# Two layers of sixteen experts: the last expert's first product moved ahead of the fifteenth's second one

## The chip, the core and the metric

The kernel runs on one core of one Trainium2 chip. The metric is the time of one execution on the device in microseconds, the median of the runs; lower is better.

## The reference

An encoder of two layers over 512 tokens of width 1024. Each layer has a mixer (attention in the first, a gated recurrence in the second), a layer norm, a mixture of experts and another layer norm. Only the experts and what follows them matter here:

```python
def grouped_moe(x, router_w, router_bias, w1, w3, w2):
    ...
    y = jnp.zeros_like(t)
    for e in range(N_EXPERTS):
        h = jax.nn.silu(t @ w1[e]) * (t @ w3[e])
        y = y + gates[:, e:e + 1] * (h @ w2[e])
    return y.reshape(bsz, seq, d)
...
        h = layer_norm(ALPHA * h + grouped_moe(h, router_w, router_bias, *experts[layer]), *norm2[layer])
```

There are 16 experts with an inner width of 512. Each token goes to two of them, so most gates are zero.

## The kernel before

**The work of one expert.** Up to 96 tokens of an expert are gathered into one tile (`gather`, L552) and transposed on PE (`x_t`). `w13` (from L570) multiplies them with W1 and W3: the "a" job, 48 matmuls of 128 x 96 against 512 columns. `glu` makes h from the two results (SiLU on ACT L594, product on DVE L595). `h_t` transposes h with four transposes on PE (L603), and writes it as a high part H (copy on ACT, L604) and the rest L (subtraction on DVE, L605). `w2` multiplies with W2: the "b" job, 24 matmuls (L629 to L631). `scatter` multiplies with the gate while it moves the result out of PSUM (y, ACT L639), and a DMA issued on POOL adds the rows to the buffer `ybuf` in DRAM (L640).

**Precision and weights.** Every product is made of three: high times high, low times high, high times low. So each weight tile of 128 x 1024 is split on the way: `wh` by a copy on ACT (L131), `wl` by a subtraction on DVE (L132). `Stream` hands out the weights in one order for the whole layer, the order in which `moe_items` lists them from `jobs()`. SP issues their loads as slots come free (`ld_a`, L681: one chunk is two transfers of 512 KB; `ld_b`, L687: one of 1 MB). An "a" job has four chunks, a "b" job two. `conv_to` converts ahead into a ring of four tile pairs and, but for the last twelve conversions of a layer, two more. Whatever its place in the list, a chunk takes the slot that its number gives.

**The order of the jobs.** Experts count from 0. `jobs()` puts the "a" job of an expert ahead of the "b" job of the expert before, so that PE has a first product to work on while h of the last one is made. Only at the end is the order turned: ..., 14a, 13b, 14b, 15a, 15b. For expert 15 `h_t` follows its "a" job at once (L755); for the others it is called behind the "b" job before. The framework makes all semaphores; it puts the instructions of each engine in order by their place in the program and by when it reckons them ready, so a transposition can stand on PE ahead of matmuls that the program has first.

```python
                if e in (0, E - 1):
                    HT[e] = self.h_t(h2, nm)
...
            py = self.w2(st, (l, e), *HT[e], nm, LA, e == E - 1)
            if e < E - 2:
                HT[e + 1] = self.h_t(hm, f"{l}_{e + 1}")
```

H and L of `h_t` have one buffer each, so a new H waits until the "b" job before has read the old one. PSUM has two buffers for the results of `w2`.

**The end of a layer.** Expert 15's result isn't scattered. `direct` multiplies it with one-hot matrices on PE (L664, L665), which brings its rows into token order in PSUM (`pd`). The results of the others come back from `ybuf`: four DMAs issued on POOL, one for each 128 tokens, add `ybuf` to the residual tile of these tokens (`xr`, L780). A scatter to `ybuf` waits for the one before to land, and these four wait for the last scatter. `tail` then adds `pd` to each of the four tiles on DVE (L801, two halves each) and normalises it: squares on ACT (L330), gain on DVE (L809, L834), the power -1/2 on POOL (L336), bias on DVE (L813) or POOL (L819). `pd` has four PSUM buffers, two row tiles' worth. In layer 0 the order on ACT and DVE in the tail is written out by hand in `TAIL`; each finished tile is transposed for layer 1 (L1054). In layer 1 each finished tile goes to the output (L1732).

`load_ln` (L317, L318) loads the gain g and the bias b of the norm on POOL's queue; they take the two extra buffers of the ring of converted weights.

Of the kernel before, what the change touches and what calls it, by code (L numbers as in the profile page):

```python
# [24 lines left out]
E = 16  # L25
# [14 lines left out]
LA = 2  # L40
# [155 lines left out]
class K:  # L196
# [408 lines left out]
        self.last_hl = nc.vector.tensor_tensor(L, pt, H.bitcast(F32), op=ALU.subtract).ins  # L605
        return H, L

    def w2(self, st, key, H, L, nm, la, last=False):
        nc = self.nc
        py = [self.ps.tile([P, 512], F32, name=f"py{nm}{n}", tag="r")[:CAP] for n in range(2)]  # L610
        mm = []
        for fc in range(FC):
            i = st.where[(key, "w2", fc // 2)] + fc % 2
            if last:
                with self.tc.issue_after(self.last_hl):
                    st.conv_to(i + 1 + la)
            else:
                st.conv_to(i + 1 + la)
            wh, wl = st.get(i)
            for n in range(2):  # L620
                sl = slice(n * 512, (n + 1) * 512)
                mm.append((n, fc))
                mm[-1] += (wh[:, sl], wl[:, sl])
            if last and fc % 2 == 0:
                continue
            if last:
                mm.sort(key=lambda x: x[0])
            for n, c, a, b in mm:
                nc.tensor.matmul(py[n], H[:, c], a, start=c == 0, stop=False)  # L629
                nc.tensor.matmul(py[n], H[:, c], b, start=False, stop=False)  # L630
                nc.tensor.matmul(py[n], L[:, c], a, start=False, stop=c == FC - 1)  # L631
            mm = []
        return py

    def scatter(self, l, py, gate, dst, nm):
# [60 lines left out]
    def jobs(self):  # L696
        r = []
        for e in range(E):
            r += [(e, "a"), (e - 1, "b")] if e < E - 1 else [(e - 1, "b"), (e, "a")]
        return r[:1] + r[2:] + [(E - 1, "b")]  # L700

    def moe_items(self, it, l):
# [6 lines left out]
    def moe(self, l, st, hs, after, on_done):  # L709
        nc, tc = self.nc, self.tc  # L710
        self.hs = hs
        self.s2 = [self.rp.tile([P, 2], F32, name=f"s2{l}{t}", tag="s1", bufs=4) for t in range(NT)]
        st.limit = st.where["moe_end", l]
        xg, X, HT, gi = {}, {}, {}, []
        seq = [e for e in range(OV + 1)] + ["o"] + [e for e in range(OV + 1, E)]

        def gather(i):
            if seq[i] == "o":
                self.thr, self.over = self.over_begin(l)
            ix = self.over[0][:, 0:1] if seq[i] == "o" else self.idx[:, seq[i]:seq[i] + 1]  # L720
            xg[seq[i]] = self.gather(ix, i)
            gi.append(self.last_gather)

        gather(0)
        port = self.rp.tile([P, 1], F32, name=f"port{l}", tag="port")
        with tc.issue_after(gi[0]):
            nc.gpsimd.memset(port, 0.0)
            gather(1)
        X[0] = self.x_t(xg[0], f"{l}_0")
        gather(NXG)  # L730
        first = st.where["moe", l]
        with tc.issue_after(self.last.ins), tc.issue_after(self.last_sig):
            free = nc.vector.tensor_copy(self.rp.tile([P, 1], F32, name=f"free{l}", tag="port"), port).ins
            with tc.issue_after(free):
                st.conv_to(first + 6)
        hm = None
        for e, what in self.jobs():
            nm = f"{l}_{e}"
            if what == "a":
                if e == OV:  # L740
                    self.over_count(l)
                pp = self.w13(st, (l, e), *X[e], nm, LA if e != OV else HX)
                if e == OV:
                    self.overflow(l, xg["o"])
                    tc.no_sync_barrier()
                h2 = self.glu(*pp, nm)
                if e == OV:
                    X[e + 1] = self.x_t(xg[e + 1], f"{l}_{e + 1}")
                elif e < E - 1:
                    with tc.issue_after(self.last_mm):  # L750
                        X[e + 1] = self.x_t(xg[e + 1], f"{l}_{e + 1}")
                if e + 1 + NXG < len(seq):
                    gather(e + 1 + NXG)
                if e in (0, E - 1):
                    HT[e] = self.h_t(h2, nm)  # L755
                hm = h2
                if 4 <= e < 4 + NT:
                    with tc.issue_after(gi[e]):
                        nc.gpsimd.tensor_scalar(hs[e - 4], hs[e - 4], ALPHA, 1.0, op0=ALU.mult, op1=ALU.mult)
                continue  # L760
            if e == E - 1:
                st.load_to(st.chunk(st.limit - 1) + 1)
                if l == 0:
                    self.early = True
                    st.load_to(st.nd + 2)
                    self.early = False
            py = self.w2(st, (l, e), *HT[e], nm, LA, e == E - 1)
            if e < E - 2:
                HT[e + 1] = self.h_t(hm, f"{l}_{e + 1}")
            if e == 0:  # L770
                with tc.issue_after(gi[1]), tc.issue_after(self.last.ins):
                    self.route_end()
            gate = self.gpos[:, e:e + 1]
            if e < E - 1:
                self.scatter(l, py, gate, self.dst[:, e:e + 1], nm)
                if e == E - 2:
                    g, b = self.load_ln(l, 2, ("vh", HX), self.hl2)
        acc = []
        for t in range(NT):
            acc.append(nc.gpsimd.dma_start(hs[t], self.ybuf[l][t * P:(t + 1) * P], accum_op=ALU.add).ins)  # L780
        after()
        done = st.limit
        st.limit = len(st.parts)
        if l == 0:
            st.conv_to(done + 2)
            with tc.manual_schedule(engines={mybir.EngineType.Activation, mybir.EngineType.DVE}):
                self.tail(l, py, gate, self.idx[:, E - 1:E], g, b, on_done, lambda n: st.conv_to(done + n))
        else:
            self.tail(l, py, gate, self.idx[:, E - 1:E], g, b, on_done)
# [967 lines left out]
```

## Time and profile before

| | us |
|---|---|
| median of 3 runs | 1131.86 |
| lowest, highest | 1131.6, 1134.7 |
| the profiled execution | 1139.46 |
| its span, first to last instruction | 1137.5 |

The profile is of one execution, somewhat slower than the median. Times in its views count from the first instruction. PE is TensorE (PEld its weight loads), ACT ScalarE, DVE VectorE, POOL GpSimd, SP the engine that issues loads. A matmul of 512 columns is shown with about 0.39 us though the next starts 0.23 us after it, since they are pipelined. In a timeline the bracket behind a row is how long the engine had been idle and what ended that; it is inferred, and a transfer that several semaphores stand for can be named wrongly. In the chain of waits "issue" is time in which the engine waited for nothing that the profile shows. The view of DMA issues gives the median time from issue to landing of the transfers that fall in its window. Layer 0's experts end at about 572 us of the span, layer 1's at about 1111.

### The profile page before, as it was taken

To read this page: it belongs to the slowest core of one execution; us is meant where nothing else is said; L and a number is where in the kernel's file an instruction comes from. 1 tells how busy PE (TensorE), PEld (TensorE's weight loads), DVE (VectorE), ACT (ScalarE), POOL (GpSimd) and SP (SyncE) were. 2 spreads that over 40 slices of the span, in tenths; PEclk is the share of its full clock that TensorE was granted. 3 is DMA by queue.
4 is the path that set the end of the run, shared out by engine and by line. 5 is a ranking of instruction groups with operands and counts; after the bars stand their busy time and mean duration, and the time that the engine had idled before them with its cause. 6 is when DMAs were issued, how large, how long until landed. Compare 5 with 4: busy or idle time off the path is not lost. (4 is left out here: it accounts for less than half of the span.)

```text
span 1137.5 us, 14945 instructions
## 1 busy us (share of the span) xinstructions
PE 1044.2 (92%) x5010; PEld 765.1 (67%) x5010; DVE 906.9 (80%) x1481; ACT 766.1 (67%) x1112; POOL 240.8 (21%) x238
## 2 busy tenths in 40 slices
PE   7999898995999999999979999995999999998992
PEld 5677677883677777776558657774677777775651
DVE  5586778558999999997886597848999999996775
ACT  5456688333878888786744899233878888786762
POOL 1113555315123111120210000014123111120132
PEclk9898999996999999999979999996999999999996
DMA  8181010696999999989953203496999999997983
GB/s 298 56 259 38 1 38 1 229 344 208 358 327 365 361 357 359 357 306 361 311 127 120 70 14 111 155 380 206 359 316 375 362 358 365 365 335 248 332 254 101
DMA packets 132980, 281.22 MB, mean 247 GB/s; under 512 B 8905, under 2 KB 32617, under 8 KB 132769
## 3 DMA queue, kind: packets, MB, share of 16 engines
q1 hardware_dynamic: 121344, 245.20, 60.0%
q0 software_dynamic: 10928, 33.93, 12.3%
q10 hardware_dynamic: 624, 1.08, 0.3%
q8 instruction: 41, 0.67, 0.2%
q14 instruction: 43, 0.34, 0.1%
HBM read 261.41 MB, written 23.74 MB: 251 GB/s over the span
## 5 line engine op out<-in xcount | busy, mean ns | idle before, releaser
L132 DVE TENSOR_TENSOR wl<-rr,wh 128x1024 fp32r<-128x1024 f32 x180 | 212.1, 1219 | 17.3 <-ACT wh L131 16.3
L131 ACT CAST wh<-rr 128x1024 fp32r<-128x1024 f32 x180 | 180.2, 1049 | 40.2 <-PE p L587 33.0
L132 DVE TENSOR_TENSOR wl<-rf,wh 128x1024 fp32r<-128x1024 f32 x104 | 124.0, 1220 | 20.8 <-ACT wh L131 20.3
L131 ACT CAST wh<-rf 128x1024 fp32r<-128x1024 f32 x104 | 105.2, 1048 | 46.6 <-DMA rf<-l_w_out 26.0
L132 DVE TENSOR_TENSOR wl<-raw,wh 128x1024 fp32r<-128x1024 f32 (+1 forms) x101 | 119.1, 1207 | 16.9 <-ACT wh L131 16.9
L131 ACT CAST wh<-raw 128x1024 fp32r<-128x1024 f32 (+1 forms) x101 | 100.9, 1033 | 30.5 <-PE ppx L1073 8.1
L583 PE MATMUL p<-wh,xh 128*96 128x512 f32 x256 | 103.3, 404 | 1.5 <-ACT xh L566 1.5
L629 PE MATMUL py<-wh,hh 128*96 128x512 f32 x256 | 101.4, 404 | 3.0 <-ACT y L639 1.9
L630 PE MATMUL py<-wl,hh 128*96 128x512 f32 x256 | 101.5, 396 | 1.6 <-DVE wl L132 1.6
L631 PE MATMUL py<-wh,hl 128*96 128x512 f32 x256 | 101.1, 398 | 0.9 <-DVE hl L605 0.9
L585 PE MATMUL p<-wh,xh 128*96 128x512 f32 x256 | 101.2, 395 | 0.3
L587 PE MATMUL p<-wh,xl 128*96 128x512 f32 x256 | 101.4, 396 | 0.0
L584 PE MATMUL p<-wl,xh 128*96 128x512 f32 x256 | 101.3, 396 | 0.0
L586 PE MATMUL p<-wl,xh 128*96 128x512 f32 x256 | 101.0, 395 | 0.0
L588 PE MATMUL p<-wh,xl 128*96 128x512 f32 x256 | 101.0, 395 | 0.0
L640 POOL DMA_INDIRECT ybuf<-y,dst x30 | 58.9, 1964 | 178.5 <-ACT y L639 151.8
L552 POOL DMA_INDIRECT xg<-hbuf,idx x32 | 35.4, 1108 | 237.3 <-PE xt L565 199.6
L132 DVE TENSOR_TENSOR wl<-rx,wh 128x1024 fp32r<-128x1024 f32 x56 | 66.3, 1219 | 8.4 <-ACT wh L131 8.4
L131 ACT CAST wh<-rx 128x1024 fp32r<-128x1024 f32 x56 | 56.2, 1050 | 9.8 <-PE p L587 9.1
L629 PEld LDWEIGHTS py<-wh,hh 128*96 128x96 f32 x256 | 41.4, 163 | 19.8 <-ACT y L639 3.4
L631 PEld LDWEIGHTS py<-wh,hl 128*96 128x96 f32 x256 | 41.7, 163 | 19.2 <-DVE hl L605 1.8
L585 PEld LDWEIGHTS p<-wh,xh 128*96 128x96 f32 x256 | 41.5, 162 | 19.3 <-ACT wh L131 1.2
(426 smaller groups left out, 2438.9 us busy)
## 6 DMA issues: line engine op xcount, KB each, us to landing
rr<-l_w SPq DMA_DIRECT2D x124, 512.0 KB, 11.3
rf<-l_w SPq DMA_DIRECT2D x68, 512.0 KB, 13.1
rr<-l_w SPq DMA_DIRECT2D x28, 1024.0 KB, 14.2
rx<-l_w SPq DMA_DIRECT2D x36, 512.0 KB, 12.0
raw<-l_w SPq DMA_DIRECT2D x36, 512.0 KB, 13.2
rf<-l_w SPq DMA_DIRECT2D x15, 1024.0 KB, 12.6
raw<-l_w SPq DMA_DIRECT2D x13, 1024.0 KB, 8.5
raw<-l_w_in SPq DMA_DIRECT2D x11, 1024.0 KB, 5.6
```

The costliest lines, as they stand in the source:

```text
L131: nc.scalar.copy(h[:, :w], r[:, a:a + w])
L132: nc.vector.tensor_tensor(l[:, :w], r[:, a:a + w], h[:, :w].bitcast(F32), op=ALU.subtract)
L583: nc.tensor.matmul(p1, H[:, kc], w1h[:, sl], start=f, stop=False)
L584: nc.tensor.matmul(p1, H[:, kc], w1l[:, sl], start=False, stop=False)
L585: nc.tensor.matmul(p3, H[:, kc], w3h[:, sl], start=f, stop=False)
L586: nc.tensor.matmul(p3, H[:, kc], w3l[:, sl], start=False, stop=False)
L587: nc.tensor.matmul(p1, L[:, kc], w1h[:, sl], start=False, stop=e)
L588: self.last_mm = nc.tensor.matmul(p3, L[:, kc], w3h[:, sl], start=False, stop=e).ins
L629: nc.tensor.matmul(py[n], H[:, c], a, start=c == 0, stop=False)
L630: nc.tensor.matmul(py[n], H[:, c], b, start=False, stop=False)
L631: nc.tensor.matmul(py[n], L[:, c], a, start=False, stop=c == FC - 1)
L640: nc.gpsimd.indirect_dma_start(out=self.ybuf[l], out_offset=bass.IndirectOffsetOnAxis(ap=dst, axis=0), in_=y, in_offset=None, bounds_check ...
```

## The change

The list of jobs keeps one order to the end: ..., 14a, 13b, 15a, 14b, 15b. Expert 15's `h_t` moves with it. It can't run ahead of 14b in the buffers of `h_t`, since expert 14's H and L are in use, so it takes the tiles of x (tags `xh` and `xl`, by the tag "x"), and it is called by a function that `w2` calls behind half of expert 14's matmuls. As the loads follow the list, the weights of 15a are loaded and converted ahead of those of 14b.

```diff
@@ w2
-    def w2(self, st, key, H, L, nm, la, last=False):
+    def w2(self, st, key, H, L, nm, la, last=False, mid=None):
...
             mm = []
+            if fc == 1 and mid:
+                mid()
         return py
@@ jobs
-            r += [(e, "a"), (e - 1, "b")] if e < E - 1 else [(e - 1, "b"), (e, "a")]
+            r += [(e, "a"), (e - 1, "b")]
         return r[:1] + r[2:] + [(E - 1, "b")]
@@ moe
-                if e in (0, E - 1):
+                if e == 0:
                     HT[e] = self.h_t(h2, nm)
...
-            py = self.w2(st, (l, e), *HT[e], nm, LA, e == E - 1)
+            def mid():
+                if e == E - 2:
+                    HT[E - 1] = self.h_t(hm, f"{l}_{E - 1}", "x")
+
+            py = self.w2(st, (l, e), *HT[e], nm, LA, e == E - 1, mid)
```

## Rows read from the trace of the kernel before

**Rows 1.** The page, busy time of each engine: us, share of the span, instructions.

```profile
PE 1044.2 (92%) x5010; PEld 765.1 (67%) x5010; DVE 906.9 (80%) x1481; ACT 766.1 (67%) x1112; POOL 240.8 (21%) x238
```

**Rows 2.** Chain that ended last, at layer 1's end: start us, us, what.

```profile
1093.69 6.23 DMA ybuf<-y,dst
1104.07 13.83 issue
```

**Rows 3.** Timeline of POOL, both layers' ends: start us, us, engine, line, what.

```profile
556.74 2.36 POOL L640 DMA_INDIRECT ybuf<-y,dst  x1 [3.04 <-ACT wh L131]
566.14 3.62 POOL L780 DMA_DIRECT2D xr<-ybuf  x4 [7.03 <-DMA ybuf<-y,dst]
...
1084.76 1.41 POOL L640 DMA_INDIRECT ybuf<-y,dst  x1 [12.92 <-DMA rr<-l_w]
1093.69 2.48 POOL L640 DMA_INDIRECT ybuf<-y,dst  x1 [2.90 <-ACT wh L131]
1100.44 3.62 POOL L780 DMA_DIRECT2D xr<-ybuf  x4 [4.27 <-DMA ybuf<-y,dst]
```

**Rows 4.** Layer 0: DMA issues, us to landing; the third accumulation's issue on POOL.

```profile
ybuf<-y,dst POOLq DMA_INDIRECT x1, 8.9
...
xr<-ybuf POOLq DMA_DIRECT2D x1, 512.0 KB, 5.4
...
567.27 2.49 POOL L780 DMA_DIRECT2D xr<-ybuf  x2
...
xr<-ybuf POOLq DMA_DIRECT2D x3, 512.0 KB, 9.4
```

**Rows 5.** The same of layer 1, ahead of them expert 13's scatter.

```profile
ybuf<-y,dst POOLq DMA_INDIRECT x1, 8.1
...
xr<-ybuf POOLq DMA_DIRECT2D x1, 512.0 KB, 5.5
...
1101.60 2.47 POOL L780 DMA_DIRECT2D xr<-ybuf  x2
...
xr<-ybuf POOLq DMA_DIRECT2D x3, 512.0 KB, 9.3
```

**Rows 6.** Timeline of DVE: first sums of the tail that use a row tile.

```profile
577.44 0.68 DVE L801 SCALAR_TENSOR_TENSOR xr<-xr,pd 128x512 f32<-128x512 f32 x1
...
1111.77 0.69 DVE L801 SCALAR_TENSOR_TENSOR xr<-xr,pd 128x512 f32<-128x512 f32 x1 [0.59 <-PE pd L665]
1115.24 0.68 DVE L801 SCALAR_TENSOR_TENSOR xr<-xr,pd 128x512 f32<-128x512 f32 x1
```

**Rows 7.** Timeline of PE, both layers' ends; in brackets idle time and its releaser.

```profile
545.61 0.39 PE L631 MATMUL py<-wh,hl 128*96 128x512 f32 x1
...
572.28 0.39 PE L664 MATMUL pd<-yh,ot 96*128 96x512 f32 x1
...
1077.29 0.47 PE L630 MATMUL py<-wl,hh 128*96 128x512 f32 x1 [0.82 <-DVE wl L132]
...
1082.64 0.39 PE L631 MATMUL py<-wh,hl 128*96 128x512 f32 x1
1083.96 0.47 PE L629 MATMUL py<-wh,hh 128*96 128x512 f32 x1 [0.93 <-ACT y L639]
...
1089.68 0.39 PE L583 MATMUL p<-wh,xh 128*96 128x512 f32 x1
...
1100.64 0.39 PE L588 MATMUL p<-wh,xl 128*96 128x512 f32 x1
1101.88 0.55 PE L603 MATMUL ht<-call,hm 96*128 96x96 f32 x4 [0.85 <-DVE hm L595]
...
1110.88 0.39 PE L664 MATMUL pd<-yh,ot 96*128 96x512 f32 x1
```

**Rows 8.** Windows of layer 1: us, busy (count) by engine, PEclk, DMA share, GB/s.

```profile
1083.00:1089.80 6.80, 5.88 (x26) 3.99 (x26) 5.67 (x6) 5.86 (x9) 2.04 (x2) 1.00 1.04 395
1105.00:1108.00 3.00, 3.00 (x8) 1.94 (x8) 1.83 (x2) 0.00 (x0) 0.00 (x0) 0.50 1.02 195
```

## The prediction

> **What bounds the kernel now.** I read the page first: PE is the busiest engine, 92% of the span [rows 1]. That is the share over the whole kernel, and it says nothing yet of a layer's end, so I went to the chain that ended last. There, at layer 1's end, it leaves PE: a transfer into `ybuf` of 6.2 us, the issue of the loads that add `ybuf` to the row tiles, and then 13.8 us in which the chain names no engine at all [rows 2]. So I followed that path by hand, with POOL's timeline and the DMA issues.
>
> The path is: y of expert 14, its scatter, the landing of that scatter, four accumulating loads (L780), and the tail's sums (L801). POOL issues the scatter at 556.74 in layer 0 and 1093.69 in layer 1, and the first accumulating load at 566.14 and 1100.44, in both cases released by the landing of that scatter [rows 3]. The scatter took 8.9 us in layer 0 [rows 4] and 6.2 in layer 1 [rows 2]; 0.5 us lie between landing and next issue. The first accumulation lands 5.4 and 5.5 us after its issue. The third is issued at 567.27 and 1101.60, 1.1 and 1.2 us after the first; the view that holds the last three gives a median, so the middle one, of 9.4 and 9.3 us [rows 4, 5]. It is there at 576.7 and 1110.9, that is 10.5 us after the first issue in both layers. The tail's sums are one row tile after the other on DVE, in a fixed order in layer 0, and the third tile's first sum runs at 577.44 and 1115.24 [rows 6]. **So the slack of this path is only 0.8 us in layer 0 and 4.3 in layer 1.** PE's path to the same sums runs through expert 15: its transposes, second product and the products `pd`, which begin at 572.28 and 1110.88 [rows 7]. In layer 1 the first sum waited for `pd` (0.59 us) while its row tile, due at 1100.44 + 5.5 = 1105.9, had been there for 5.9 us [rows 3, 5, 6].
>
> **The change part by part.** *What goes.* Expert 15's transposes no longer stand behind its own first product. In layer 1, PE idles 0.85 us before them and the whole step takes from 1100.64 to beyond 1101.88 + 0.55 [rows 7]. Expert 14's second product no longer waits 0.93 us behind expert 13's for y to leave PSUM [rows 7], since expert 15's first product stands between them.
>
> *What moves.* Expert 14's second product (24 matmuls), and with it its y, its scatter and all that waits for that, go behind expert 15's first product (48). In expert 15's, 47 steps take 1100.64 - 1089.68 = 10.96 us, 0.233 each [rows 7]. After the last matmul of expert 13 at 1082.64 come 72 matmuls (16.8 us), and four transposes (0.55 at most), so the last matmul of expert 14 is issued at 1100.0 if nothing waits. It will wait: at the head of expert 15's first product for conversions that ACT begins only after y and the copy of H, and at the head of expert 14's second for a conversion behind SiLU and the gate product. The nearest row of the second kind is the 0.82 us at 1077.29, behind expert 14's first product; there eight transposes of x stood in front, which nothing replaces now (by the four at 1101.88 up to 1.1 us, so up to 1.9 in all). The nearest of the first kind is the 0.93 us at 1083.96 [rows 7], with two conversions already done in both cases. The lower end is no wait at all, since the conversions may be ahead: 0 to 2.8 us. I take 0.9 for the second, as in its row, and 0.5 for the first, half of its row: 1.4. From the last matmul to the scatter's issue expert 13 needs 1084.76 - 1082.64 = 2.1 us [rows 3, 7], with the copy of H ahead of y; here that copy is done earlier, so 1.6 to 2.1, and I take 1.8. The scatter is then issued at 1100.0 + 1.4 + 1.8 = 1103.2, **9.5 us later than now** (7.9 to 11.2). In layer 0 the same count from 545.61 gives 566.2, 9.4 later than 556.74.
>
> *What hides it.* Now the scatter has a start of one whole first product on the tail, and that cover is what the change takes. A wait that goes with it doesn't help: expert 13's scatter lands 8.1 us after 1084.76, at 1092.9, and that is what holds expert 14's until 1093.69, though the releasers named there are a conversion and a weight [rows 3, 5]; after the change it has long landed, and the 9.5 us have that in them.
>
> *Layer 0.* The scatter took 8.9 us beside the loads of the next weights, and 6.2 in layer 1 where these had ended [rows 2, 4]. Ten us later the loads have ended here too, so I take 7.0 (6.2 to 8.9). Landing 573.2, first issue 573.7, third tile 584.2: the third tile's sum goes from 577.44 to 584.2, **6.8 us later**. With both ends (issue 564.5 and landing after 6.2; 567.9 and 8.9) it is 4.2 to 10.4. What stands behind that sum on DVE, the first normalised tile and layer 1's first products, follows in the same order, and I take the delay as handed on in full.
>
> *Layer 1.* Scatter 6.2 us, landing 1109.4, first issue 1109.9, third tile 1120.4 instead of 1115.24: **5.1 us later**. At the low end DVE fills its wait for the third tile with the normalisation of the first; then only the first tile's slack counts: 1101.6 + 6.2 + 0.5 + 5.5 = 1113.8 against 1111.77, 2 us. At the high end (issue 1104.9, landing after 8.9) it is 9.6.
>
> *What costs nothing.* The transposes in the middle of expert 14's second product: ACT's copy and DVE's subtraction have the other half of that product as cover; without it they would be the wait that stands there now. Expert 15's H and L go into the tiles of x, free once its first product has ended. SP's queue: expert 15's four chunks of W1 and W3 (eight transfers) go ahead of expert 14's two of W2, of the same size, into slots that come free at the same places; what covers this is their lead: PE's waits here name ACT and DVE, none a transfer [rows 7], and if it failed one landing would come on top of the 1.4 us. POOL's queue: the loads of g and b come free by the same places in the stream of conversions as now, and stay ahead of the scatter; the four accumulations stay behind it, and nothing else waits on POOL but the tail's small powers, which are later with everything.
>
> The sum is 6.8 + 5.1 = 11.9 us. The profiled execution took 1139.46, so it would take 1151.4; the median of the runs lies 7.6 us lower, so 1131.86 + 11.9 = 1143.8.
>
> One price I weigh against a rule. While only the accumulations run the DMA engines are full (share 1.02) at 195 GB/s, where weight loads moved 395 [rows 8]; I take the 195, because it is this transfer at this place. The Trainium skill (DMA: Bandwidth & Descriptors, Anatomy of one DMA) gives a fixed 2.0 us and 436 GB/s instead: three loads would then be an estimated 5.6 us, and the sum 2.1 instead of 11.9. The rows' 10.5 us disagree with it.
>
> **The rivals.** *PE sets the end, and it gets faster.* Expert 15's second product would begin with no transposes, copy or subtraction before it. By the count above `pd` begins at 1100.2 + 1.4 + 24 x 0.233 + 0.5 (half of the 0.93, y alone) = 1107.7 instead of 1110.88, and in layer 0 at 570.7 instead of 572.28; together 4.8 us, time 1127.1. Part of it is the clock: from 1105 to 1108, behind the idle stretches, it was granted at 0.50, the 1.2 GHz level [rows 8]. The Trainium skill (TensorE: Matmul & The Clock Gate, Why this matters for your kernels) asks to leave no idle gaps between bursts of matmuls, which speaks for this change. This rival decides only if the scatter and three accumulations took under 9 us after 1103.2, not the 17 that they take. 0.09.
>
> *The accumulations are fast when alone.* If they moved at the 395 GB/s of the weight loads, the third would be there 2.8 us (5.5 less 0.52 MB at 195 GB/s) + 3 x 1.33 = 6.8 after the first issue instead of 10.5, and each layer would lose 3.7 less: 1136.4, slower still. The Trainium skill's rule above would make that 1134.0. For it speaks that the engines can move twice as much; against it, that the accumulations had them to themselves from 1105 to 1108, with the weights in. 0.04.
>
> *The order on PE does not change*, because instructions are put on a queue by readiness as well as by place. Then expert 14's scatter stays where it is, 1131.9. Against it: expert 14's second product and expert 15's first now stand on PE in the order of the program, 1083.96 and 1089.68 [rows 7]. 0.07.
>
> **How the numbers follow.** About 0.3% (3.4 us) is what a measurement can tell from no change. My case has 0.80, all of it slower by over 0.3%; its low ends of both layers give 1138 (4.2 + 2.0) and its high ends 1152 (10.4 + 9.6), and as two high ends hardly fall together I stop at 1150. Fast accumulations add 0.04 to slower: 0.84. No change has 0.07, faster 0.09. The range reaches down to 1134, past the fast accumulations, and leaves out the faster case and most of no change.
>
> **What would show it.** In the changed trace: the scatter of expert 14 issued near 566 and, with the delay of layer 0 taken off, 1103; accumulations issued some 7 us after it and landing 2.5 us apart; the tail's first sums waiting for a DMA and no longer for `pd`; PE idle before `pd` of the third tile; expert 15's second product at one pace, begun at once. I am wrong if the accumulations land before `pd` is there, or if the third tile's sum in layer 0 is less than 3 us later.

## The result, and the profile after

| | before | after |
|---|---|---|
| median, us | 1131.73 (1131.44 to 1134.7, 4 runs) | 1146.24 (1143.57 to 1149.06, 4 runs) |
| ratio, after to before | | 1.0105 (95%: 1.0068 to 1.0142) |
| the profiled execution, span | 1137.5 | 1141.6 |

The change makes the kernel slower, by 1.05% (11.9 us of 1131.7; the interval is 7.7 to 16.1). The ratio is not the quotient of the two medians, which lie 14.5 us apart. The prediction was 1143.8, 11.9 more than the median shown to it.

The two spans can't be set against each other as they stand: the place of the change is reached at different times (layer 0's expert 13 ends at 545.61 in the profile of before [rows 7], at 540.98 in that of after, and between 540.2 and 546.0 in all profiles of the study, with either order). So every time below is counted **from the last matmul of expert 13's second product** in its layer.

The page, busy time of each engine, first row as in [rows 1]. PE is busy for 4 us less (a second profile of the kernel before has 1041.4, so 2.8 of them need no edit) and the kernel is slower, so PE's share of 91% again says nothing about the layer's end:

```profile
PE 1040.0 (91%) x5010; PEld 762.2 (67%) x5010; DVE 906.5 (79%) x1481; ACT 765.9 (67%) x1112; POOL 241.0 (21%) x238
```

POOL's timeline at both layers' ends (start us, us, engine, line, what; in brackets idle time and its releaser). It answers to [rows 3]:

```profile
542.87 1.43 POOL L642 DMA_INDIRECT ybuf<-y,dst  x1 [17.89 <-ACT y L641]
...
561.54 1.54 POOL L642 DMA_INDIRECT ybuf<-y,dst  x1 [13.01 <-ACT y L641]
567.41 3.62 POOL L786 DMA_DIRECT2D xr<-ybuf  x4 [4.33 <-DMA ybuf<-y,dst]
...
1087.43 1.41 POOL L642 DMA_INDIRECT ybuf<-y,dst  x1 [14.95 <-DMA rf<-l_w]
...
1105.96 1.56 POOL L642 DMA_INDIRECT ybuf<-y,dst  x1 [12.87 <-ACT y L641]
1111.84 3.62 POOL L786 DMA_DIRECT2D xr<-ybuf  x4 [4.32 <-DMA ybuf<-y,dst]
```

Expert 14's scatter now follows expert 13's by 18.7 us (561.54 - 542.87), where it followed by 9.0 (556.74 [rows 3] - 547.73; in layer 1 by 8.9 [rows 3]). In layer 0 the accumulating loads start 26.4 us after expert 13's last matmul (567.41 - 540.98) instead of 20.5 (566.14 - 545.61).

DMA issues (us from issue to landing) in layer 0: the scatter of 14, the load of the next mixer's weights issued at 566.88, and the first accumulating load; then the first one of layer 1. They answer to [rows 4, 5]:

```profile
ybuf<-y,dst POOLq DMA_INDIRECT x1, 5.3
...
raw<-l_w_in SPq DMA_DIRECT2D x1, 1024.0 KB, 5.8
...
xr<-ybuf POOLq DMA_DIRECT2D x1, 512.0 KB, 8.0
...
xr<-ybuf POOLq DMA_DIRECT2D x1, 512.0 KB, 5.4
```

The scatter is faster than in either layer before (8.9 and 6.2 us), the first accumulation of layer 0 slower (8.0 instead of 5.4). What stands beside it is the load of `l_w_in`. The view of the DMA queues (packets, MB, share of the 16 DMA engines' time; q1 carries SP's loads, q0 what POOL issues) has from 569 to 571.5 us that load alone:

```profile
q1 hardware_dynamic: 732, 0.75, 99.8%
```

So the accumulation, issued at 567.41, moves nothing until the load is nearly through; in layer 1, with nothing beside it, its first packets go under 2 us after its issue. In the kernel before the two stand the other way round. There the same load is issued at 572.49, behind the four accumulations, and it is the load that takes long (9.7 us to landing instead of 5.8):

```profile
raw<-l_w_in SPq DMA_DIRECT2D x1, 1024.0 KB, 9.7
```

DVE's timeline, the tail's sums (L807) and, in layer 1, the gain of the first tile (L815). It answers to [rows 6]:

```profile
575.52 0.69 DVE L807 SCALAR_TENSOR_TENSOR xr<-xr,pd 128x512 f32<-128x512 f32 x1 [7.35 <-DMA xr<-ybuf]
...
577.98 0.69 DVE L807 SCALAR_TENSOR_TENSOR xr<-xr,pd 128x512 f32<-128x512 f32 x1 [0.90 <-DMA xr<-ybuf]
...
580.50 0.69 DVE L807 SCALAR_TENSOR_TENSOR xr<-xr,pd 128x512 f32<-128x512 f32 x1 [0.92 <-DMA xr<-ybuf]
...
602.10 1.29 DVE L1064 TENSOR_TENSOR x<-ftm,x 128x512 fp32r<-128x512 f32 x2 [3.82 <-ACT x L1063]
...
1117.33 0.69 DVE L807 SCALAR_TENSOR_TENSOR xr<-xr,pd 128x512 f32<-128x512 f32 x1 [4.88 <-DMA xr<-ybuf]
...
1119.74 0.69 DVE L807 SCALAR_TENSOR_TENSOR xr<-xr,pd 128x512 f32<-128x512 f32 x1 [0.86 <-DMA xr<-ybuf]
...
1120.97 1.28 DVE L815 SCALAR_TENSOR_TENSOR xr<-xr,lw,g 128x1024 f32<-128x1024 f32 x1
...
1122.35 0.68 DVE L807 SCALAR_TENSOR_TENSOR xr<-xr,pd 128x512 f32<-128x512 f32 x1
```

This view has the main result. Before, the first sum waited for `pd`, in layer 1 for 0.59 us [rows 6] and in layer 0 for 0.50:

```profile
574.45 0.69 DVE L801 SCALAR_TENSOR_TENSOR xr<-xr,pd 128x512 f32<-128x512 f32 x1 [0.50 <-PE pd L665]
```

Now it waits 7.35 us in layer 0 and 4.88 us in layer 1 for a row tile to come back from `ybuf`, and in layer 0 the second and third sum wait again, 2.5 us apart, the pace at which the accumulations land. In layer 1 DVE takes the first tile's gain ahead of the third tile's sum, so that sum waits for nothing.

PE's timeline, which answers to [rows 7]:

```profile
540.98 0.39 PE L631 MATMUL py<-wh,hl 128*96 128x512 f32 x1
...
553.44 0.70 PE L629 MATMUL py<-wh,hh 128*96 128x512 f32 x2 [0.33 <-ACT wh L131]
553.98 0.53 PE L603 MATMUL ht<-call,hm 96*128 96x96 f32 x4
555.09 0.47 PE L630 MATMUL py<-wl,hh 128*96 128x512 f32 x1 [0.58 <-DVE wl L132]
...
560.02 0.39 PE L631 MATMUL py<-wh,hl 128*96 128x512 f32 x1
560.73 0.47 PE L629 MATMUL py<-wh,hh 128*96 128x512 f32 x1 [0.32 <-ACT y L641]
...
566.36 0.49 PE L666 MATMUL pd<-yh,ot 96*128 96x512 f32 x1
...
576.27 0.80 PE L666 MATMUL pd<-yh,ot 96*128 96x512 f32 x1 [7.11 <-DVE xr L807]
...
1085.55 0.39 PE L631 MATMUL py<-wh,hl 128*96 128x512 f32 x1
...
1110.80 0.50 PE L666 MATMUL pd<-yh,ot 96*128 96x512 f32 x1
```

PE has done what the change wants: short gaps (0.32 to 0.58 us), expert 15's second product right behind expert 14's. But then it idles 7.11 us before `pd` of the third row tile, whose PSUM buffer the first tile's sum has to free. Windows of PE's clock (us, busy and count by engine, PEclk, DMA share, GB/s): layer 0 while only the accumulating loads move, then the restart in layer 1's mixer, then layer 1's last products, which answer to the last of [rows 8]:

```profile
572.60:580.40 7.80, 3.75 (x8) 2.31 (x8) 3.10 (x11) 2.03 (x3) 0.57 (x1) 0.50 1.07 211
...
592.30:598.30 6.00, 6.00 (x27) 5.78 (x28) 5.97 (x7) 2.31 (x3) 0.00 (x0) 0.50 0.01 3
598.30:604.00 5.70, 5.70 (x50) 5.70 (x49) 1.90 (x3) 1.07 (x2) 0.55 (x1) 1.00 1.01 351
...
1105.00:1108.00 3.00, 2.85 (x12) 2.02 (x13) 1.96 (x3) 2.56 (x4) 1.56 (x1) 1.00 0.00 0
```

Before, the same restart stood at the 1.2 GHz level for 3.2 us only; the same view of before:

```profile
589.20:592.40 3.20, 3.20 (x13) 2.98 (x14) 3.20 (x4) 2.33 (x3) 0.00 (x0) 0.50 0.00 0
592.40:598.00 5.60, 5.60 (x49) 5.60 (x48) 2.91 (x5) 0.74 (x2) 0.55 (x1) 0.98 0.50 148
```

And DVE's timeline of before, the landmark that answers to 602.10 above:

```profile
597.88 1.29 DVE L1058 TENSOR_TENSOR x<-ftm,x 128x512 fp32r<-128x512 f32 x2 [2.69 <-ACT x L1057]
```

**Where the time went.** In layer 0 the third tile's sum goes from 31.83 us (577.44 - 545.61 [rows 6, 7]) to 39.52 (580.50 - 540.98): 7.7 later. By the third tile's features in the next mixer, a landmark behind the slow clock, it is 52.27 (597.88 - 545.61) to 61.12 (602.10 - 540.98): 8.85. The 1.15 between them is the clock's: 27 matmuls ran at the low level instead of 13. An estimate from the windows, 14 matmuls at 6.00 / 27 = 0.22 us instead of 5.70 / 50 = 0.11, gives 1.5 us; it is somewhat high, since short transposes are among the 50. In layer 1 the third tile's sum is 4.2 later (32.60 to 36.80), but the end of the span only 1.2 (54.86 to 56.05). Both are larger against a second profile of the kernel before, 5.8 (from 31.01) and 2.7 (from 53.33); why is said under "Both kernels again".

### The profile page after: what moved, and what is told of

Same layout as the page of the kernel before. It is cut to its first block, busy times and chain, and to the rows that moved or that the text cites. A ratio compares the mean times of both kernels' runs of the same rounds, so it can differ in the third digit from the quotient of the medians.

```text
span 1141.6 us, 14949 instructions
## 1 busy us (share of the span) xinstructions
PE 1040.0 (91%) x5010; PEld 762.2 (67%) x5010; DVE 906.5 (79%) x1481; ACT 765.9 (67%) x1112; POOL 241.0 (21%) x238
## 5 line engine op out<-in xcount | busy, mean ns | idle before, releaser
L629 PE MATMUL py<-wh,hh 128*96 128x512 f32 x256 | 99.1, 401 | 1.4 <-ACT wh L131 0.8
L585 PEld LDWEIGHTS p<-wh,xh 128*96 128x96 f32 x256 | 41.6, 163 | 20.4 <-ACT wh L131 2.4
L630 PEld LDWEIGHTS py<-wl,hh 128*96 128x96 f32 x256 | 41.3, 161 | 19.7 <-DVE wl L132 4.6
L583 PEld LDWEIGHTS p<-wh,xh 128*96 128x96 f32 x256 | 41.6, 163 | 18.4 <-ACT xh L566 2.4
## 6 DMA issues: line engine op xcount, KB each, us to landing
rr<-l_w SPq DMA_DIRECT2D x30, 1024.0 KB, 14.3
raw<-l_w SPq DMA_DIRECT2D x36, 512.0 KB, 13.1
rf<-l_w SPq DMA_DIRECT2D x15, 1024.0 KB, 12.5
```

Source lines behind the costliest of these rows:

```text
L583: nc.tensor.matmul(p1, H[:, kc], w1h[:, sl], start=f, stop=False)
L585: nc.tensor.matmul(p3, H[:, kc], w3h[:, sl], start=f, stop=False)
```

## The experiments

The table has all the kernels that ran, each beside runs of the kernel before on the same chip. "Layer 0" is the time from expert 13's last matmul to the third tile's features (L1058 of before), "layer 1" that from expert 13's last matmul to the end of the span, each of the profiled execution. Layer 1's 1.5 us of spread in the order of before (53.3 to 54.9) is there without any edit. The kernel before gave 1.0019 against itself, so a ratio this close to 1 says little.

| kernel | median, us | ratio to before (95%) | layer 0 | layer 1 |
|---|---|---|---|---|
| before, the first profile | | | 52.27 | 54.86 |
| before again | 1137.6 | 1.0019 (0.9997 to 1.0040) | 52.77 | 53.33 |
| after, the first profile | 1146.24 | 1.0105 (1.0068 to 1.0142) | 61.12 | 56.05 |
| after again | 1149.06 | 1.0128 (1.0092 to 1.0164) | 61.13 | 56.40 |
| layer 0 alone | 1148.03 | 1.0110 (1.0083 to 1.0137) | 60.94 | 54.92 |
| layer 1 alone | 1137.58 | 1.0027 (1.0005 to 1.0049) | 52.28 | 56.40 |
| no scatter of 14 | 1133.35 | 0.9984 (0.9958 to 1.0011) | 58.01 | 50.07 |
| before, accumulations late | 1147.8 | 1.0129 (1.0082 to 1.0176) | 61.70 | 57.25 |
| transposes behind 14b | 1148.33 | 1.0120 (1.0076 to 1.0164) | 60.94 | 56.42 |
| third w_in load behind | 1140.56 | 1.0053 (1.0032 to 1.0074) | 58.40 | 53.27 |
| the same again | 1138.62 | 1.0031 (1.0018 to 1.0044) | 58.29 | 53.27 |
| both experts on PE | 1137.84 | 1.0022 (1.0004 to 1.0040) | 52.50 | 52.10 |
| both on PE, loads gated | 1132.47 | 0.9976 (0.9962 to 0.9991) | 52.49 | 52.13 |

### Both kernels again

No edit; the two show what a repeat is worth.

> The kernel before, unchanged. It measures how far two sets of runs of one kernel lie apart and gives a second profile of it. Theory (the 4.1 us between the two profiled spans is too little because the first profiled execution of before lost 5 us in its first 130 us): ratio 1.000 within 0.3%, and a span near 1130, with the third row tile's sum of layer 0's tail at most 1 us behind the landing of its accumulation. Rival (the tail's times in that execution were untypical too): the tail's sums stand elsewhere against the last matmul of expert 13 than 31.8 us (layer 0) and 32.6 us (layer 1).

> The changed kernel, unchanged. Theory (a late scatter of expert 14 in both layers): 1.008 to 1.013 times the kernel before, and again the first sums of both tails wait for an accumulation, the scatter issued 20.5 us after the last matmul of expert 13. Rival (its slower runs are another effect, for instance of the clock): the time moves by over 0.4% from run to run with the tails unchanged.

The difference stands: 1.0019 against 1.0128. Before and after lie 8.4 to 8.9 us apart in layer 0, by which pair of profiles is taken, and 1.2 to 3.1 in layer 1. The span of before was not near 1130, as was expected, but 1135.4; its expert 13 too ends late in layer 0, at 545.94.

The rival of the first expectation holds for layer 1: there the third tile's sum comes 31.01 us after expert 13's last matmul, not 32.6, and `pd` begins after 26.67 us instead of 28.24. That is PE's clock. The stretch that stood at 0.50 in the first profile [rows 8] is granted 1.00 in this one, behind the same three gaps on PE (0.85, 0.57 and 0.45 us):

```profile
1105.00:1108.00 3.00, 3.00 (x14) 2.09 (x13) 1.26 (x2) 0.43 (x1) 0.00 (x0) 1.00 1.07 206
```

So the first profile's figures for layer 1, on which the prediction rests too, have some 1.5 us of slow clock in them that this kernel does not always have.

### One layer at a time

`jobs` takes the layer and keeps the old end of the list in the other one (shown for layer 0 alone):

```diff
-            r += [(e, "a"), (e - 1, "b")]
+            r += [(e, "a"), (e - 1, "b")] if e < E - 1 or l == 0 else [(e - 1, "b"), (e, "a")]
...
-                if e == 0:
+                if e == 0 or (e == E - 1 and l != 0):
...
-                if e == E - 2:
+                if e == E - 2 and l == 0:
```

> The new order in layer 0 alone, layer 1 as before. Theory from the changed trace (layer 0 loses 7.7 us in its tail and 1.1 us behind it): 1131.7 + 8.8 = 1140.5. Rival, the terms as they were forecast (6.8): 1138.5. Rival, the loss is shared evenly by the layers: 1139. A time within 2 us of the whole change would say that layer 1's end costs nothing.

> The new order in layer 1 alone, layer 0 as before. Theory from the changed trace (the third row tile's sum is 4.2 us later, of which the tail takes back all but 1.2): 1132.9. Rival, the forecast term (5.1 us, the tail handing it on): 1136.8. Rival (PE's gain of 3 us reaches the end): 1128.7.

Layer 0 alone has all of the loss that a ratio can show (1.0110 of 1.0105 to 1.0128), layer 1 alone 0.27%, with an interval that begins just above none, and the kernel before gave 0.19% against itself. The traces order the layers in the same way: +8.2 to +8.7 us in layer 0, +1.5 to +3.1 in layer 1. The ratio of layer 0 alone is more than that, 12.5 us (9.4 to 15.5) where 8.8 were expected; where the rest lies was not found out.

### No scatter of expert 14

```diff
-                self.scatter(l, py, gate, self.dst[:, e:e + 1], nm)
+                self.scatter(l, py, gate, self.dst[:, e:e + 1], nm, e != E - 2)
...
+        if not send:
+            return
```

> The order after, with the scatter of expert 14's rows left out (its two products and the scaling of y stay, so TensorE does the same work; the output lacks expert 14's rows). Theory (the wait for the scattered rows 14 is the whole loss): the accumulating loads wait for expert 13's scatter alone, which is issued some 20 us before 14's was, so the first sum of the tail waits for TensorE's pd instead of the accumulations: DVE's 7.35 us wait (layer 0) and 4.88 us wait (layer 1) are gone, the tail's sums start near 568 and 1113 us on the clock of the profile after, and the time falls to or a little under the kernel before: ratio to the kernel before 0.995 to 1.000. Rival (the new order itself costs time on TensorE, by its three short gaps per layer or its clock): the ratio stays at 1.010 to 1.013.

The ratio falls to 0.9984: **with TensorE's order that of after, the kernel as a whole loses nothing once nothing waits for that scatter.** So the order on PE isn't the cause. In the profile of layer 0, though, most of the loss is still there, by another wait: the sums don't begin near 568 us, as was expected. POOL, ACT, PE and DVE of that kernel, in that order:

```profile
551.61 3.59 POOL L788 DMA_DIRECT2D xr<-ybuf  x4 [3.09 <-DMA ybuf<-y,dst]
...
568.89 1.99 ACT L131 CAST wh<-raw 128x1024 fp32r<-128x1024 f32 x2 [5.77 <-DMA raw<-l_w_in]
570.78 1.25 ACT L660 ACTIVATE yh<-py,gpos 96x512 fp32r<-96x512 f32 x2
...
571.52 2.22 PE L668 MATMUL pd<-yh,ot 96*128 96x512 f32 x4 [5.04 <-ACT yh L660]
...
574.20 0.69 DVE L809 SCALAR_TENSOR_TENSOR xr<-xr,pd 128x512 f32<-128x512 f32 x1 [0.56 <-PE pd L669]
```

The wait that was taken away made room for another one. The accumulations, issued at 551.61, now move beside the two `w_in` loads that were issued at 537 and 540. From 558 to 568 us the queues of that kernel moved:

```profile
q0 software_dynamic: 490, 1.75, 87.9%
q1 hardware_dynamic: 380, 0.38, 13.5%
```

The plain loads, which have the engines nearly to themselves in the window above from after, get 13.5% here. ACT waits 5.77 us for the first of them, and behind that conversion on ACT's queue stands yh, without which PE can't begin `pd`. Layer 0 is 58.0 instead of 52.3; layer 1, which has no such loads, is 50.1, 3.3 to 4.8 us shorter than before, and the two nearly cancel. The profiled execution is the second slowest of the ten (1137.62, median 1133.35), so ACT's wait may be less in others. That layer 0 loses nothing with PE's new order and no scatter of 14 is seen in the kernels with both experts on PE, below: 52.5.

### The order of before, with late accumulations

A second scatter, of a tile of zeros to the same rows, behind that of expert 14:

```diff
+        if again:
+            z = self.wp.tile([CAP, D], F32, name="yz" + nm, tag="y", bufs=3)
+            nc.vector.memset(z, 0.0)
+            nc.gpsimd.indirect_dma_start(
+                out=self.ybuf[l], out_offset=bass.IndirectOffsetOnAxis(ap=dst, axis=0), in_=z, in_offset=None,
+                bounds_check=S + CAP - 1, oob_is_err=True, compute_op=ALU.add)
```

> The order before, with one scatter more: a tile of zeros added to expert 14's rows behind the scatter of 14, so that the accumulating loads start some 5 to 9 us later (one scatter took 5.4 to 8.9 us) while TensorE's order is that of before. Theory (a late start of the accumulations is what costs): the third tile's sum of layer 0, which had 0.8 us to spare, comes 4 to 8 us later, that of layer 1, with 4.3 us to spare and a tail that can put other work ahead, 0 to 2 us, and the clock of the next stage gives up to 1 us more: ratio to the kernel before 1.004 to 1.009. Rival (order on TensorE is the cause): ratio 0.998 to 1.002.

POOL and DVE of that kernel:

```profile
561.95 1.81 POOL L646 DMA_INDIRECT ybuf<-yz,dst  x1 [7.38 <-DVE wl L132]
568.05 3.64 POOL L786 DMA_DIRECT2D xr<-ybuf  x4 [4.29 <-DMA ybuf<-yz,dst]
...
576.50 0.69 DVE L807 SCALAR_TENSOR_TENSOR xr<-xr,pd 128x512 f32<-128x512 f32 x1 [7.20 <-DMA xr<-ybuf]
```

This is the loss without the change: the jobs stand in the order of before, the accumulations start 27.0 us after expert 13's last matmul (568.05 - 541.04; 26.4 in after), DVE waits 7.20 us, and the ratio is after's, 1.0129. The mechanism is what was expected; the size was put too low (1.004 to 1.009), because here too the first accumulation took over 8 us (568.05 to 576.50) instead of 5.4, beside a load of `w_in` that was issued at 567.85.

### Transposes behind expert 14's second product

```diff
-            py = self.w2(st, (l, e), *HT[e], nm, LA, e == E - 1, mid)
+            py = self.w2(st, (l, e), *HT[e], nm, LA, e == E - 1)
+            mid()
```

> The order after, with expert 15's transposes behind the whole of 14b, as in the order of the other experts, not in its middle. Theory (TensorE does not set the end, the accumulating loads do): 15b and pd come about 1.5 to 2.5 us later in each layer, which stays inside the 7.35 and 4.88 us that DVE waits for the loads: the time is that of after, ratio to the kernel before 1.009 to 1.014, and the waits shrink by what pd is later. Rival (TensorE sets the end): 3 to 5 us more than after, ratio 1.013 to 1.017.

The time is after's, but that tells nothing of PE: the transposes (L603) stand at 12.99 us from expert 13's last matmul here and at 13.00 in after (553.98 - 540.98), at the head of 14b in both. Their place on PE is not set by where the program calls them. So the test doesn't tell the theories apart; it is one more repeat of after. That the diff's "middle" isn't where they run is read from the timeline above.

### The next mixer's load behind the accumulations

The third chunk of `w_in` goes on POOL's queue, behind the four accumulating loads:

```diff
-                nc.sync.dma_start(t.rearrange("p (a b) -> p a b", a=KC),
+                q = nc.gpsimd if c0 == D + 512 else nc.sync
+                q.dma_start(t.rearrange("p (a b) -> p a b", a=KC),
...
             st.conv_to(done + 2)
+            self.early = True
+            st.load_to(st.nd + 1)
+            self.early = False
```

> The order after, with the third chunk of the next mixer's weights (1 MB) sent from GpSimd's queue behind the four accumulating loads of layer 0, instead of from SyncE's queue, where it was issued at 566.88 us and moved beside them. Theory (that load is why layer 0's first accumulation took 8.1 us from its issue where it takes 5.4 us alone): DVE's wait of 7.35 us in layer 0 shrinks to 4.5 to 5.2 us, the third tile's sum comes 2 to 3 us earlier, and the time is 2 to 3 us under after: ratio to the kernel before 1.006 to 1.011. Rival (the accumulations are slow there of themselves, after the scatter): the wait stays over 7 us and the ratio is after's, 1.010 to 1.013. Layer 1 is not touched.

> The same kernel as the one with the third w_in load behind the accumulations, once more: its time stood 6 to 8 us under after's by the ratios, while the traces show 2.7 us of it in layer 0. If the trace has it all, the ratio to before is 1.007 to 1.010; if the earlier ratio holds, 1.003 to 1.0075.

POOL and DVE of layer 0:

```profile
568.45 3.65 POOL L786 DMA_DIRECT2D xr<-ybuf  x4 [4.52 <-DMA ybuf<-y,dst]
570.66 2.39 POOL L915 DMA_DIRECT2D raw<-l_w_in  x1
...
573.98 0.69 DVE L810 SCALAR_TENSOR_TENSOR xr<-xr,pd 128x512 f32<-128x512 f32 x1 [4.95 <-DMA xr<-ybuf]
```

With the load out of the way the first accumulation is there after 5.5 us (568.45 to 573.98, was 8.1), DVE's wait is 4.95 instead of 7.35, and layer 0 is 2.7 us shorter. **So the loads of the next stage are why layer 0's accumulations were slower than before.** In the kernel before, the same chunk was issued at 572.49, 6.3 us behind the first accumulation; from expert 13's last matmul that is 26.9 us, against 25.9 in after. The change moves the accumulations, hardly the load, and so puts them side by side. The Trainium skill (DMA: Bandwidth & Descriptors, Queues, rings and completion order) says that each DMA engine takes turns between the queues that have work for it. By that both transfers should be late; the rows show it for one only, the one that came second: in after the accumulation (8.0 instead of 5.4), while the load took 5.8, against a median of 5.7 for the eight loads of its line; in before the load (9.7). In the run without the scatter, where both have long been under way, the queues sent 490 and 380 packets in the same time; that looks like turns, with more bytes and far more time for a packet of an accumulation.

The ratio fell by more than 2.7 us: 1.0053 and 1.0031 against 1.0105 and 1.0128. Of what is left, 3.0 us lie at the very end. The last instruction on DVE:

```profile
1131.22 1.28 DVE L822 SCALAR_TENSOR_TENSOR xr<-xr,lw,b 128x1024 f32<-128x1024 f32 x1 [0.66 <-POOL lw L336]
```

The row ahead is DVE's timeline; the span and clock of the core are:

```profile
core 0: 1136.5 us, clock 0.960
```

From there to the end it is 5.3 us, in both profiles of this kernel; in after it is 8.3 us (1133.29 to 1141.6), and so, within 0.5 us, in all other kernels of the study. What shortens it was not found out; the load on POOL's queue alone doesn't, since the gated kernel below has it too and ends 8.2 us behind.

### Both experts on PE

Expert 14's result goes the way of expert 15's: split, and added by one-hot products into the same `pd`. No scatter of 14, and no row left out:

```diff
-                self.scatter(l, py, gate, self.dst[:, e:e + 1], nm)
+                if e < E - 2:
+                    self.scatter(l, py, gate, self.dst[:, e:e + 1], nm)
+                else:
+                    self.d14 = self.direct(py, gate, self.idx[:, e:e + 1], nm, 0)
...
-                nc.tensor.matmul(ps, oh[:, t], yH[:, sl], start=True, stop=False)
-                nc.tensor.matmul(ps, oh[:, t], yL[:, sl], start=False, stop=True)
+                for i, (oh, yH, yL) in enumerate(parts):
+                    nc.tensor.matmul(ps, oh[:, t], yH[:, sl], start=i == 0, stop=False)
+                    nc.tensor.matmul(ps, oh[:, t], yL[:, sl], start=False, stop=i == len(parts) - 1)
```

The second of the two kernels also holds layer 0's accumulations until both `w_in` loads have landed, and has the third `w_in` load on POOL's queue, as above:

```diff
+            gate_ins = nc.gpsimd.tensor_tensor(lit, st.raw[c0][:, 0:1], st.raw[c0 + 1][:, 0:1], op=ALU.add).ins
+        with tc.issue_after(gate_ins):
             for t in range(NT):
                 acc.append(nc.gpsimd.dma_start(hs[t], self.ybuf[l][t * P:(t + 1) * P], accum_op=ALU.add).ins)
```

> The order after, with expert 14's rows brought in the same way as expert 15's: its y split into a high and a low part and added by one-hot products on TensorE into the same pd, and no scatter of 14 (16 matmuls more per layer; every row is computed). Theory: the accumulating loads of layer 0 start near 551 us, as in the run without the scatter, and there collide with the two w_in loads that were issued at 537 and 540 us, so ScalarE's conversion of w_in waits and holds yh and pd back behind it (5.8 us in that run): DVE's wait for xr is gone, one for PE of 4 to 7 us stands in its place, and the time is that of the kernel before plus up to 4 us for the 16 matmuls per layer: ratio 0.998 to 1.004. Rival (the accumulations were the only thing in the way, and the collision is an accident of one execution): pd starts at 566 to 568 us and the ratio is 0.994 to 0.998.

> As the kernel with both experts on TensorE, and in layer 0 the accumulating loads are held on GpSimd until the two w_in loads have landed (a one-column add that reads both), and the third w_in load goes behind them on the same queue. Theory: w_in lands at 557 to 560 us as in after, the conversion and yh are not held, the accumulations run alone from about 560 us (first sum possible at 565.5, third at 570.6), pd comes at 566.5 to 569: no wait over 2 us is left on DVE in front of the tail's sums, the third tile's sum comes 0 to 2.5 us earlier than in before against the last matmul of 13b: ratio to the kernel before 0.995 to 1.000. Rival (something else holds the tail: the 16 matmuls more, or DVE's extra split of y for expert 14, 2 x 0.7 us, ahead of weight conversions): ratio 1.001 to 1.006.

POOL and DVE of the gated one, layer 0:

```profile
560.66 0.18 POOL L805 TENSOR_TENSOR landed<-raw,raw 128x1 f32<-128x1 f32 x1 [12.90 <-DMA raw<-l_w_in]
561.14 3.64 POOL L808 DMA_DIRECT2D xr<-ybuf  x4 [0.30 <-POOL landed L805]
...
569.14 0.69 DVE L833 SCALAR_TENSOR_TENSOR xr<-xr,pd 128x512 f32<-128x512 f32 x1
...
572.22 0.68 DVE L833 SCALAR_TENSOR_TENSOR xr<-xr,pd 128x512 f32<-128x512 f32 x1
```

No sum waits for a DMA any more, and at 0.9976 this version beats before and after. Its gain isn't where it was expected: the third tile's sum of layer 0 comes 31.98 us after expert 13's last matmul (572.22 - 540.24), as before (31.83), and the 1.2 to 2.7 us are in layer 1 (52.13). Without the gate the ratio is 1.0022, within what was expected. Its accumulations, too, move beside the `w_in` loads (14.3 us from issue to landing in the median), but the wait that was to explain the ratio is not in its profile: ACT waits for no `w_in` there, and its two stages are as long as the gated one's. That profile is of the fastest of its six executions (1132.31, median 1137.84). The 0.46% between these two is thus open; the 5.77 us wait of the run without the scatter is one candidate, if it comes in some executions and not in others.

## Why the prediction was right

**The path, right.** The prediction followed y of 14, scatter, landing, four accumulations, sums. Taking the scatter away takes the loss away (0.9984 in all; in layer 0 by the kernels with both experts on PE, 52.5), and delaying the accumulations alone, with the old order, brings it about (1.0129). The first rival, PE sets the end, falls with these two; but its arithmetic held: `pd` begins 25.25 us after expert 13's last matmul in layer 1 (1110.80 - 1085.55) and 25.38 in layer 0, where it said 25.1 for both. The 4.8 us that it gave to PE are simply not on the path. Layer 1's last products ran at the 2.4 GHz level now (1.00 from 1105 to 1108, where it was 0.50 [rows 8]). The Trainium skill's wish for no idle gaps (TensorE: Matmul & The Clock Gate, Why this matters for your kernels) would have that so, but no run here shows that the change did it: the second profile of the kernel before has the gaps and 1.00 as well. In the old order the stretch is slow in two profiles of four, in the new one in none of seven.

**When the scatter is issued, right.** "9.5 us later than now", 20.56 us after expert 13's last matmul: measured 20.56 in layer 0 (561.54 - 540.98) and 20.41 in layer 1. The parts differ a little. The last matmul of 14b comes 19.04 us after that point, where 18.8 was said; from there to the scatter it is 1.52, not 1.8. That the parts add up so well is luck: the 0.5 us of wait at the head of 15a did not come, but 15a itself took 0.4 to 0.6 longer. The transposes of expert 15 ran at the head of 14b, not in its middle, as their call has it; their cover was only longer by that.

**The scatter, too slow in the sum.** Layer 0 was given 7.0 us and took 5.3; layer 1 was given 6.2 and took 5.4. It had the DMA engines to itself in both.

**The accumulations of layer 0, too fast in the sum: the mis-sized term.** The prediction took 10.5 us from the first issue to the third tile, from the rows of before. It was 13.1 (567.41 to 580.50), because a load that had been behind them was now beside them. The step that missed it is the one on SP's queue: it followed the two experts' own loads and not what the next stage loads into the slots as they come free. The two errors partly cancel, which is luck: the third tile's sum came 7.7 us later, where 6.8 was said (4.2 to 10.4).

**Handed on in full, right for layer 0 and short of it.** Behind the sum the clock took another 1.15 us, for which the sum had no term: more matmuls at 1.2 GHz when layer 1's mixer begins. That PE's long wait in the tail makes them more is argued, not shown: the kernel before took 0.5 us more there in its second profile without any such wait.

**Layer 1, wrong in the way of its own low end.** 5.1 us were taken. The third tile's sum came 4.2 later in the first pair of profiles and 5.8 against the second profile of before: the slack of 4.3 us was in part the slow clock's. But DVE had put the first tile's gain into the wait, as the low end said it might, and the end came 1.2 us later in the first pair of profiles, 3.1 at most in others. The low end's 2 us was the better value.

**Sum.** 8.4 to 8.9 and 1.2 to 3.1 make 9.5 to 11.9 us in the traces, against 11.9 predicted: two terms off in opposite ways, so that the total is closer than its parts, by luck. The median, 1146.24, lies 2.4 us above the forecast, and the ratios (11.9 and 14.5 us) at or above what the two stages show; no stage was found for the rest.

**The accumulations' price.** Three loads took 10.5 us before and 13.1 after. By the Trainium skill (DMA: Bandwidth & Descriptors, Anatomy of one DMA) they would take an estimated 5.6 us, and the loss would have been small; the rows differ, and the measured price was the right one to use.

## What to carry to other kernels

Before work is moved later on a busy engine, follow what its result feeds to the end, through stores and loads too: here 9.4 us of delay met 0.8 us of slack, and the busy engine gained nothing by it. When a transfer moves in time, list what else is in flight at its new place; the same load took 5.4 us alone and 8.0 behind a weight load, and taking one wait away started a transfer early enough to move beside two others and, in one profile, to hold up what waited for them. In layer 0, where the order behind it is fixed, the delay was handed on in full; in layer 1, where DVE could put other ready work first, the slack of the first tile was the better guide than that of the third.

## What had not been expected

- An accumulating load of 512 KB that reads DRAM and adds to SBUF took 5.4 us from issue to landing alone, and 8.0 us beside a plain load of 1 MB that had been issued 0.5 us ahead of it and took its usual 5.8. With the accumulations ahead, in the kernel before, they took their usual time and the plain load 9.7. Where four of them met two plain loads under way, they took 13.0 us in the median and left the plain loads 13.5% of the DMA engines' time.
- PE's clock stayed at the low level for 27 matmuls of the next mixer instead of 13, so that a delay of 7.7 us became one of 8.85. PE had waited 7.11 us in one piece in the tail before it; whether that is the cause is not shown.
- From the last DVE instruction to the end of the program it is 8.2 to 8.8 us in all kernels but one, where it is 5.3 in two profiles out of two. The cause is open.
